# FFN output projection in three passes: each pass scaled and added onto the residual rows in DRAM by adding DMAs, in place of load, sum and store of a running sum

## The chip, the core and the metric

The kernel runs on one core of one Trainium2 chip. The metric is the device time of one execution in microseconds (us); lower is better. The engines are named as in the profile: PE (matrix multiplication, PEld its weight loads), DVE (vector), ACT (scalar, activation), POOL (GpSimd) and SP (which here only issues DMAs). DMAs issued on SP use the hardware queue q1, DMAs issued on POOL the software queue q0; both are carried out by the same 16 DMA engines.

## The reference

One layer of a decoder trunk on 512 tokens of width 2048, in float32. Its feed-forward half is what the change touches:

```
h   = rmsnorm(x, ffn_norm_g)               # x: the residual after the attention half, "x1"
hid = h @ w_ffn_in                         # 2048 -> 2 x 5632
x   = x + (silu(gate) * up) @ w_ffn_out    # 5632 -> 2048; the result is "x2"
ple = p @ w_ple
x   = x + sigmoid(rmsnorm(x, ple_norm_g) @ w_ple_gate) * ple
```

## The kernel before

Everything is held transposed, features on the 128 partitions and the 512 tokens along the free dimension. A row tile is 128 x 1024 float32 (512 KB): two blocks of 128 features. The residual x has 8 such tiles (`KU` = 8, index j), the hidden activations 22 (index u).

**Matmuls.** Each float32 operand is split into a high and a low part in fp32r, and each product is three matmuls (high x high, high x low, low x high). Two neighbouring units of 256 x 256 features can be multiplied by a Strassen scheme with 7 products ("S") or plainly with 8 ("P"). `pair(forms, ...)` computes one output row tile j from a list of operand forms: it takes the weights of one or two units at a time (`next_weights`), multiplies, and collects the result from the PSUM banks. `Pair.mix` and `mix_doubled` (L721, L754) combine the seven products into a `wide()` tile named `out` (two buffers, `bufs=2`) while the last unit runs. `Pair.out()` returns that tile (for pairs of plain units alone, it copies two PSUM banks into it on ACT, L792; for mixed pairs, it joins two PSUM banks on DVE, L799). `Pair.onto(h)` adds the result onto a tile h on DVE instead (L804 from `out`, or L808 twice straight from PSUM for plain pairs).

**Weights.** `Weights` loads the four blocks of an S unit by two SP DMAs (L329, L331), forms two differences by an adding DMA on POOL (L351, 256 KB, from DRAM onto SBUF), sums on DVE (L363) and splits into high parts on ACT (`whi`, L347) and low parts on DVE (`wlo`, L344). P units come by one SP DMA (L327). Four landing buffers and three slots of split weights turn round. The order is set by `tick()`, a small planner that is called twice per double unit: `after(n, fn)` runs fn n ticks later.

**Forms.** The operands on the moving side are forms: a row tile is loaded (L504), split on ACT (L274) and DVE (L275), with sums on DVE (L513). The raw tiles are blocks of one arena, `wholes`; the split forms live in an arena `parts` with room for eight S forms. A form of the next pass can be built only where both have room, and it is fetched from DRAM when `wholes` has. The engines' order in the built program follows from a list scheduler that honours these steps.

**The feed-forward output.** The hidden size is 5632, that is 22 units, too many forms for `parts`, so `w_ffn_out` is applied in three passes c = 0, 1, 2 over 8, 8 and 6 units (`PASSES`). In each pass, j runs over the 8 output tiles; at j = 0 (all units) and j = 1 (half of them, or in the last pass all four S units) units run as plain ones while the rest of their forms is still built. Between the passes the running sum of tile j is kept in DRAM (`spill["sum", j]`): pass 0 stores it (SP, L1436); pass 1 loads it, adds with `onto`, and stores it (L1441); pass 2 loads it and tile j of x1, adds with `onto`, scales the sum by the norm's row `row2` with `scaled` (DVE, L1224), adds x1 (DVE, L1444), stores x2 (L1445) and adds its squares to the next norm (`norm3.add`: ACT L956, DVE L960). The x2 tiles are loaded again as forms of the last stage, the gate (`w_gate`).

Of the kernel before, what the change touches and what calls it, by code (L numbers as in the profile page):

```python
# [12 lines left out]
F32 = mybir.dt.float32  # L13
F32R = mybir.dt.float32r
AF = mybir.ActivationFunctionType
ALU = mybir.AluOpType
# [3 lines left out]
P = 128  # L20
# [12 lines left out]
PASSES = "SSSSSSSS", "SSSSSSSS", "SSSSPP"  # L33
# [34 lines left out]
def hybrid_layer(  # L68
# [18 lines left out]
    nc = tc.nc  # L87
# [9 lines left out]
    def nm(s):  # L97
        return f"{s}_{next(names)}"
# [14 lines left out]
    class Arena:  # L113
# [5 lines left out]
        def take(self, n, how="low"):  # L119


            spots = []
            for start, size in self.holes:
                end = start + size
                if how == "place":
                    start = -(-start // (2 * PLACE)) * 2 * PLACE
                if end - start >= n:
                    if how == "high":
                        spots.append((-end, end - n))
                    elif how != "old":  # L130
                        spots.append((start, start))
                    else:
                        spots.extend((self.given[a // P : -(-(a + n) // P)].max(), a)
                                     for a in {*range(start, end - n + 1, 256), end - n})
            at = min(spots)[1]
            start, size = next(h for h in self.holes if h[0] <= at < h[0] + h[1])
            self.holes.remove((start, size))
            self.holes.extend(
                h for h in ((start, at - start), (at + n, start + size - at - n)) if h[1])
            return Block(self, at, n)  # L140

        def give(self, block):
            self.turns += 1
            self.given[block.start // P : -(-(block.start + block.n) // P)] = self.turns
            holes = sorted(self.holes + [(block.start, block.n)])
            self.holes = holes[:1]
            for s, n in holes[1:]:
                if sum(self.holes[-1]) == s:
                    self.holes[-1] = (self.holes[-1][0], self.holes[-1][1] + n)
                else:  # L150
                    self.holes.append((s, n))
# [42 lines left out]
    def after(n, fn):  # L194
        heapq.heappush(waiting, (clock[0] + n, next(names), fn))
# [306 lines left out]
    def load(src, n=1024, how="old"):  # L502
        b = take(n, how)
        nc.sync.dma_start(out=b.f(0, 1024), in_=src)  # L504
        return b
# [304 lines left out]
    def pair(forms, last=False, j=0, until=None, parts_done=None, at=0,  # L810
             home=lambda: None, doubled=0):

        until = until or (0,) * len(forms)
        kinds = now("".join(f.kind for f in forms), until, j)
        p = Pair(kinds, home, doubled)
        for k, n in doubles(kinds, at):
            slot, ws = next_weights()
            fs = forms[k : k + n]  # L820
            p.add(kinds[k], ws, [f.plain() if j < until[k] else f.get() for f in fs])
            for f, m in zip(fs, until[k : k + n]):
                if j == m - 1:
                    f.use_plain()
                if last:
                    f.free()
            slots.append(slot)
            if parts_done and k + n == kinds.find("P"):
                last_parts(p, forms[k + n :], parts_done)
                break  # L830
        return p
# [390 lines left out]
    def scaled(o, row):  # L1222
        b = o.rearrange("p (b t) -> p b t", t=T)
        nc.vector.tensor_tensor(out=b, in0=b, in1=row.unsqueeze(1).to_broadcast([P, 2, T]),  # L1224
                                op=ALU.mult)
# [10 lines left out]
    def block(w, i):  # L1236

        if w == "k":
            return a_tile("k", 1024)
        if w == "s":  # L1240
            y_a[i] = take(1024)
            return y_a[i].f()
# [56 lines left out]
    for n, ((w, i), pr) in enumerate(zip(order, made())):  # L1299
# [6 lines left out]
        o = pr.out(block(w, i) if n < 3 else None)  # L1306
# [29 lines left out]
    for j in range(KU):  # L1336
        for b in "ba":
# [9 lines left out]
            pr = pair([ys[b, i] for i in range(4)], last=j == KU - 1)  # L1347
# [4 lines left out]
            else:  # L1352
# [5 lines left out]


    norm2 = Norm()  # L1360
    spill = {(n, j): tc.dram_tile([P, 1024], F32, name=nm(n)) for n in ("x1", "sum", "x2")
             for j in range(KU)}
    there = set()

# [7 lines left out]
    for j in range(KU):  # L1372
# [5 lines left out]
        pr = pair(ms, last=j == KU - 1)  # L1378
# [3 lines left out]
        h = raw.popleft()  # L1382
# [13 lines left out]
    hs = []  # L1396
# [13 lines left out]
    for m in range(KH):  # L1410
        if m == KH - 1:
            builds.extend(hs[0])
        o = pair(fs, last=m == KH - 1, j=m, until=(1,) * KU, doubled=7).out()
        if m == 0:
            row2 = norm2.row()
# [6 lines left out]
    norm3 = Norm()  # L1422
    at = 0
    for c, units in enumerate(hs):
        first, at = at, at + len(units)
        if c == len(hs) - 1:
            builds.extend(gs)
        for j in range(KU):
            if j == KU - 1 and c < len(hs) - 1:
                builds.extend(hs[c + 1])  # L1430
            before = load(spill["sum", j]) if c else None
            x1 = load(spill["x1", j]) if c == len(PASSES) - 1 else None
            pr = pair(units, last=j == KU - 1, j=j, until=PLAIN_UNTIL[c], at=first,
                      doubled=7)
            if before is None:
                nc.sync.dma_start(out=spill["sum", j], in_=pr.out())  # L1436
                continue
            h = before.f()
            pr.onto(h)
            if x1 is None:  # L1440
                nc.sync.dma_start(out=spill["sum", j], in_=h)  # L1441
            else:
                scaled(h, row2)
                nc.vector.tensor_tensor(out=h, in0=h, in1=x1.f(), op=ALU.add)  # L1444
                nc.sync.dma_start(out=spill["x2", j], in_=h)  # L1445
                there.add(("x2", j))
                norm3.add(before)
                give(x1)
            give(before)


    for j in range(KU):
        e, x2 = load(ple_spill[j]), load(spill["x2", j])
# [21 lines left out]
        else:  # L1475
            o = pair(gs, j=j, until=GATE_UNTIL).out()
# [90 lines left out]
```

## Time and profile before

| | |
|---|---|
| median of 3 runs | 2690.93 us (2689.34 to 2696.23) |
| the profiled execution | 2691.74 us, of which the span of the instructions is 2690.0 us |
| mean granted clock of PE | 0.998 |
| PE busy | 2653.3 us, 99% of the span |
| DVE busy | 2207.7 us, 82% |
| ACT busy | 1388.7 us, 52% |
| POOL busy | 458.2 us, 17% |
| DMA | 548.62 MB moved |

By the times of its `sum` stores and loads, pass 0 of the FFN output runs from about 2060 to 2225 us of the span, pass 1 to about 2395, pass 2 to about 2525; the gate follows to the end at 2690. A busy PE in these tables is one that has a matmul in flight; the time in which it has none is what the waits of PE list. Lines such as L1224 are line numbers of the kernel before; the changed kernel's lines behind L1428 are some numbers lower.

### The profile page before, as it was taken

To read this page: it belongs to the slowest core of one execution; us is meant where nothing else is said; L and a number is where in the kernel's file an instruction comes from. 1 tells how busy PE (TensorE), PEld (TensorE's weight loads), DVE (VectorE), ACT (ScalarE), POOL (GpSimd) and SP (SyncE) were. 2 spreads that over 40 slices of the span, in tenths; PEclk is the share of its full clock that TensorE was granted. 3 is DMA by queue.
4 is the path that set the end of the run, shared out by engine and by line. 5 is a ranking of instruction groups with operands and counts; after the bars stand their busy time and mean duration, and the time that the engine had idled before them with its cause. 6 is when DMAs were issued, how large, how long until landed. Compare 5 with 4: busy or idle time off the path is not lost.

```text
span 2690.0 us, 42553 instructions
## 1 busy us (share of the span) xinstructions
PE 2653.3 (99%) x15496; PEld 2325.7 (86%) x15496; DVE 2207.7 (82%) x3715; ACT 1388.7 (52%) x2161; POOL 458.2 (17%) x549
## 2 busy tenths in 40 slices
PE   8999999999999999999999999999999999999999
PEld 7889898889898889988888888888888888888898
DVE  8687878787887666688898888888899889889876
ACT  7656565655554334375444444444445444444543
POOL 0223323232220000001111111111110111100010
PEclk9999999999999999999999999999999999999999
DMA  7677777777776457667888888888888979978884
GB/s 226 154 185 175 182 173 184 172 183 198 174 187 196 140 164 211 178 210 198 230 212 213 204 202 200 201 206 199 207 197 244 259 213 279 259 254 259 257 248 126
DMA packets 288241, 548.62 MB, mean 204 GB/s; under 512 B 25888, under 2 KB 138272, under 8 KB 288032
## 3 DMA queue, kind: packets, MB, share of 16 engines
q1 hardware_dynamic: 229232, 441.03, 50.3%
q0 software_dynamic: 58800, 104.88, 25.2%
q8 instruction: 121, 1.98, 0.3%
q14 instruction: 88, 0.72, 0.1%
HBM read 498.63 MB, written 47.19 MB: 203 GB/s over the span
## 4 chain that ended last, share of the span: by engine, by line
PE 85%; DVE 7%; DMA 3%; ACT 2%; issue 2%; POOL 1%; SPq 0%; DVEq 0%; ACTq 0%; POOLq 0%
PE ps L695 47%; PE ps L285 10%; PE ps L286 10%; PE ps L284 10%; PE small L695 6%; DVE wlo L344 2%; DVE out L754 1%; DMA wholes<-x 1%; DVE parts L275 1%; PE small L1157 1%; DMA wholes<-hid 1%; DVE wholes L363 1%; ACT whi L347 1%; DVE wholes L513 1%; PE small L1032 1%
## 5 line engine op out<-in xcount | busy, mean ns | idle before, releaser
L695 PE MATMUL ps<-parts,whi 128*128 128x512 f32 x3960 | 1324.8, 397 | 0.3 <-DVE p L754 0.3
L347 ACT ACTIVATE whi<-wholes 128x512 fp32r<-128x512 f32 (+3 forms) x933 | 866.0, 942 | 787.0 <-DVE wholes L363 274.0
L344 DVE TENSOR_TENSOR wlo<-wholes,whi 128x512 fp32r<-128x512 f32 (+3 forms) x933 | 974.1, 1078 | 85.6 <-ACT whi L347 85.4
L695 PEld LDWEIGHTS ps<-parts,wlo 128*128 128x128 f32 x3960 | 743.7, 188 | 168.1 <-issue 1.0
L695 PE MATMUL ps<-parts,wlo 128*128 128x256 f32 x3960 | 784.3, 279 | 0.1
L285 PE MATMUL ps<-parts,whi 128*128 128x256 f32 (+1 forms) x2070 | 679.5, 329 | 4.8 <-DVE parts L275 4.7
L284 PE MATMUL ps<-parts,whi 128*128 128x256 f32 (+1 forms) x2048 | 668.1, 328 | 12.4 <-ACT parts L274 10.6
L286 PE MATMUL ps<-parts,wlo 128*128 128x256 f32 (+1 forms) x2070 | 677.6, 329 | 1.7 <-DVE wlo L344 1.7
L695 PEld LDWEIGHTS ps<-parts,whi 128*128 128x128 f32 x3960 | 637.8, 189 | 5.9 <-issue 1.0
L285 PEld LDWEIGHTS ps<-parts,whi 128*128 128x128 f32 x2070 | 393.6, 190 | 46.5 <-DVE parts L275 7.3
L284 PEld LDWEIGHTS ps<-parts,whi 128*128 128x128 f32 x2048 | 388.5, 190 | 48.9 <-ACT parts L274 12.7
L286 PEld LDWEIGHTS ps<-parts,wlo 128*128 128x128 f32 x2070 | 393.5, 190 | 36.2 <-DVE wlo L344 3.2
L363 DVE TENSOR_TENSOR wholes<-wholes 128x256 f32<-128x256 f32 (+1 forms) x806 | 338.9, 420 | 19.1 <-issue 1.7
L754 DVE TENSOR_TENSOR out<-out,ps 128x256 f32<-128x256 f32 x460 | 190.8, 417 | 150.9 <-ACT out L751 150.2
L351 POOL DMA_DIRECT2D wholes<-w_ffn_in x172 | 150.1, 872 | 689.1 <-DVE wholes L363 251.7
L351 POOL DMA_DIRECT2D wholes<-w_in x132 | 118.3, 898 | 484.4 <-DMA wholes<-w_in 133.7
L695 PE MATMUL small<-parts,whi 128*128 128x512 f32 x440 | 174.5, 397 | 0.0
L275 DVE TENSOR_TENSOR parts<-wholes,parts 128x1024 fp32r<-128x1024 f32 (+4 forms) x134 | 131.0, 989 | 17.6 <-ACT parts L274 17.6
L274 ACT ACTIVATE parts<-wholes 128x1024 fp32r<-128x1024 f32 (+4 forms) x134 | 112.9, 865 | 46.9 <-DVE wholes L513 26.1
L351 POOL DMA_DIRECT2D wholes<-w_ffn_out x64 | 55.8, 872 | 402.5 <-DMA wholes<-w_ffn_out 101.6
L751 ACT ACTIVATE out<-ps 128x256 f32<-128x256 f32 x243 | 91.4, 385 | 47.5 <-PE ps L695 44.0
L1403 ACT ACTIVATE out<-out 128x512 f32<-128x512 f32 x44 | 27.9, 633 | 156.3 <-DVE out L1402 156.3
(120 smaller groups left out, 1721.6 us busy)
## 6 DMA issues: line engine op xcount, KB each, us to landing
wholes<-w_ffn_in SPq DMA_DIRECT2D x172, 384.0 KB, 5.6
wholes<-w_in SPq DMA_DIRECT2D x132, 384.0 KB, 5.0
wholes<-w_ffn_in SPq DMA_DIRECT2D x172, 256.0 KB, 4.8
wholes<-w_ffn_in POOLq DMA_DIRECT2D x172, 256.0 KB, 5.5
wholes<-w_in SPq DMA_DIRECT2D x132, 256.0 KB, 4.2
wholes<-w_in POOLq DMA_DIRECT2D x132, 256.0 KB, 4.9
wholes<-w_ffn_out SPq DMA_DIRECT2D x64, 384.0 KB, 5.4
wholes<-hid SPq DMA_DIRECT2D x42, 512.0 KB, 5.8
```

The costliest lines, as they stand in the source:

```text
L274: return (nc.scalar.activation(hi, src, AF.Copy), nc.vector.tensor_tensor(out=lo, in0=src, in1=hi.bitcast(F32), op=ALU.subtract))
L275: nc.vector.tensor_tensor(out=lo, in0=src, in1=hi.bitcast(F32), op=ALU.subtract))
L284: nc.tensor.matmul(ps, sh, mh, start=start, stop=False)
L285: nc.tensor.matmul(ps, sh, ml, start=False, stop=False)
L286: return nc.tensor.matmul(ps, sl, mh, start=False, stop=stop)
L344: in_turn(nc.vector.tensor_tensor(out=self.lo[:, blocks], in0=r, in1=h.bitcast(F32), op=ALU.subtract))
L347: in_turn(nc.scalar.activation(h, r, AF.Copy))
L351: nc.gpsimd.dma_start(out=raw[:, 3:5], in_=self.src[:, 1:3], accum_op=ALU.add)
L363: in_turn(nc.vector.tensor_tensor(out=o, in0=x, in1=y, op=ALU.add))
L695: m = nc.tensor.matmul(out, l, r, start=first and k == 0, stop=last and k == 1)
L751: in_turn(nc.scalar.activation(out, x, AF.Copy, scale=scale))
L754: in_turn(nc.vector.tensor_tensor(out=out, in0=x, in1=y, op=op))
```

## The change

Since the scale `row2` is the same for every pass, each pass's own result can be scaled and added to x1. There is no `sum` tile any more. In passes 0 and 1, the result `o` of tile j is scaled in place in its `out` buffer, and two ticks later a POOL DMA adds it onto x1's tile j in DRAM (512 KB, from SBUF onto DRAM). In pass 2, tile j of x1 (which now holds the first two passes) is loaded, the scaled result is added to it on DVE, and the rest is as before.

```diff
@@ spill
-    spill = {(n, j): tc.dram_tile([P, 1024], F32, name=nm(n)) for n in ("x1", "sum", "x2")
+    spill = {(n, j): tc.dram_tile([P, 1024], F32, name=nm(n)) for n in ("x1", "x2")
              for j in range(KU)}
@@ for c, units in enumerate(hs): ... for j in range(KU):
-            before = load(spill["sum", j]) if c else None
-            x1 = load(spill["x1", j]) if c == len(PASSES) - 1 else None
+            end = c == len(hs) - 1
+            h = load(spill["x1", j]) if end else None
             pr = pair(units, last=j == KU - 1, j=j, until=PLAIN_UNTIL[c], at=first,
                       doubled=7)
-            if before is None:
-                nc.sync.dma_start(out=spill["sum", j], in_=pr.out())
+            o = pr.out()
+            scaled(o, row2)
+            if not end:
+                after(2, lambda o=o, j=j: nc.gpsimd.dma_start(
+                    out=spill["x1", j], in_=o, accum_op=ALU.add))
                 continue
-            h = before.f()
-            pr.onto(h)
-            if x1 is None:
-                nc.sync.dma_start(out=spill["sum", j], in_=h)
-            else:
-                scaled(h, row2)
-                nc.vector.tensor_tensor(out=h, in0=h, in1=x1.f(), op=ALU.add)
-                nc.sync.dma_start(out=spill["x2", j], in_=h)
-                there.add(("x2", j))
-                norm3.add(before)
-                give(x1)
-            give(before)
+            nc.vector.tensor_tensor(out=h.f(), in0=h.f(), in1=o, op=ALU.add)
+            nc.sync.dma_start(out=spill["x2", j], in_=h.f())
+            there.add(("x2", j))
+            norm3.add(h)
+            give(h)
```

On POOL, before, the 64 adding DMAs of `w_ffn_out`'s weights stand in one row:

```order
L351 DMA wholes<-w_ffn_in 128x512 x172
L351 DMA wholes<-w_ffn_out 128x512 x64
```

With the change, the adds onto x1 (named `x_<number>`; L1438 is the new line) stand between them, here those of the first five tiles of pass 0:

```order
L351 DMA wholes<-w_ffn_in 128x512 x172
L351 DMA wholes<-w_ffn_out 128x512 x5
L1438 DMA x_823_9210<-out_18831 128x1024
L351 DMA wholes<-w_ffn_out 128x512 x4
L1438 DMA x_824_9211<-out_18901 128x1024
L351 DMA wholes<-w_ffn_out 128x512 x3
L1438 DMA x_825_9212<-out_19175 128x1024
L351 DMA wholes<-w_ffn_out 128x512 x4
L1438 DMA x_826_9213<-out_19351 128x1024
L351 DMA wholes<-w_ffn_out 128x512 x4
L1438 DMA x_827_9214<-out_19527 128x1024
```

Sixteen DMAs of 512 KB are thus queued on POOL among the weights' own adds, about one for every four of these.

On ACT, at the start of pass 2, before (`parts` are the forms' high parts, `whi` the weights'; L956 is the square of tile 1 for the norm, L718 a step of `mix` of tile 2):

```order
L347 ACTIVATE whi_78<-wholes 128x1024
L274 ACTIVATE parts<-wholes 128x4x256
L347 ACTIVATE whi_76<-wholes 128x1280
L956 ACTIVATE out_21774<-wholes 128x1024
L274 ACTIVATE parts<-wholes 128x4x256 x2
L718 ACTIVATE out_21839<-ps_21781 128x512
L347 ACTIVATE whi_76<-wholes 128x512
L718 ACTIVATE out_21839<-ps_21794 128x512
```

and with the change (L792 copies tile 1's PSUM banks into `out`):

```order
L508 ACTIVATE wholes<-wholes,gcol 128x512 x2
L274 ACTIVATE parts<-wholes 128x4x256
L792 ACTIVATE out_21774<-ps_21660 128x512
L347 ACTIVATE whi_78<-wholes 128x1024
L792 ACTIVATE out_21774<-ps_21661 128x512
L508 ACTIVATE wholes<-wholes,gcol 128x512 x2
L347 ACTIVATE whi_76<-wholes 128x1280
L956 ACTIVATE out_21780<-wholes 128x1024
L718 ACTIVATE out_21845<-ps_21786 128x512
L347 ACTIVATE whi_76<-wholes 128x512
L718 ACTIVATE out_21845<-ps_21799 128x512
```

The two form splits (`128x4x256 x2`) that stood directly behind the square of tile 1 are no longer there, and two copies of PSUM banks have come in ahead of it.

On SP, at the step from pass 1 to pass 2, before (`hid` tiles are numbered in the order of the units; 10849 is the last unit, u = 21, and 10844 is u = 16, the first of pass 2, whose second load this is; an S form is loaded twice, once for its plain part and once for its sums):

```order
L327 DMA wholes<-w_ffn_out 128x1024 x2
L504 DMA wholes<-hid_10848 128x1024
L504 DMA wholes<-sum_9218 128x1024
L327 DMA wholes<-w_ffn_out 128x1024
L329 DMA wholes<-w_ffn_out 128x2x256
L331 DMA wholes<-w_ffn_out 128x768
L504 DMA wholes<-x_823_9210 128x1024
L1441 DMA sum_9225<-wholes 128x1024
L329 DMA wholes<-w_ffn_out 128x2x256
L331 DMA wholes<-w_ffn_out 128x768
L504 DMA wholes<-hid_10849 128x1024
L504 DMA wholes<-hid_10844 128x1024
```

and with the change (the numbers are 8 lower, since the 8 `sum` tiles are gone: 10841 is u = 21, 10837 to 10839 are u = 17 to 19):

```order
L327 DMA wholes<-w_ffn_out 128x1024 x5
L504 DMA wholes<-hid_10837 128x1024
L504 DMA wholes<-x_823_9210 128x1024
L327 DMA wholes<-w_ffn_out 128x1024
L329 DMA wholes<-w_ffn_out 128x2x256
L331 DMA wholes<-w_ffn_out 128x768
L504 DMA wholes<-hid_10840 128x1024
L504 DMA wholes<-hid_10841 128x1024
L504 DMA wholes<-hid_10838 128x1024
L329 DMA wholes<-w_ffn_out 128x2x256
L331 DMA wholes<-w_ffn_out 128x768
L504 DMA wholes<-hid_10839 128x1024
```

The stores and loads of `sum` are gone. The second loads of u = 17, 18 and 19 now stand here, about four weight loads earlier than before, and that of u = 16 stands in the middle of pass 1; the loads of u = 20 and 21 stand next to each other at nearly the place where u = 21 stood.

## The prediction

> **What bounds the kernel now.** I read the page first, then the windows of the FFN output and the gate, then the waits of PE, and last the timeline at the gaps of PE.
>
> ```profile
> PE 2653.3 (99%) x15496; PEld 2325.7 (86%) x15496; DVE 2207.7 (82%) x3715; ACT 1388.7 (52%) x2161; POOL 458.2 (17%) x549
> 2060.00:2225.00 165.00, 164.99 (x922) 143.12 (x921) 145.50 (x251) 82.60 (x109) 22.69 (x26) 1.00 0.87 254
> 2225.00:2395.00 170.00, 166.53 (x925) 143.53 (x924) 149.69 (x251) 77.53 (x102) 22.69 (x26) 1.00 0.89 260
> 2395.00:2600.00 205.00, 197.16 (x1218) 177.94 (x1218) 176.61 (x261) 107.39 (x138) 21.41 (x23) 0.98 0.85 261
> ```
>
> The windows give span, PE, PEld, DVE, ACT, POOL, clock, DMA share and GB/s. PE bounds the kernel: it is busy for 99% of the span. In pass 0 (the first window) it never stops, in pass 1 it loses 3.5 us, from pass 2 on more. The change touches no matmul, so whatever it gains or loses must pass through the time in which PE has nothing to do. That time, from the start of pass 0 to the end of the kernel, stands in the waits of PE (us in total, times, longest):
>
> ```profile
> PE ps L284 <- ACT parts L274: 5.3, 4, 2.0
> PE ps L285 <- DVE parts L275: 4.2, 4, 2.0
> PE ps L286 <- DVE wlo L344: 1.0, 1, 1.0
> PE small L944 <- DVE diag L942: 0.8, 1, 0.8
> ```
>
> 11.3 us in all, and 9.5 of them are waits for forms (L274, L275), not for weights. PE's gaps at the step from pass 1 to pass 2, and the one wait for weights, in the timeline (start, duration, and in brackets the idle time before):
>
> ```profile
> 2390.92 0.73 PE L284 MATMUL ps<-parts,whi 128*128 128x512 f32 x2 [1.52 <-ACT parts L274]
> 2419.66 0.62 PE L284 MATMUL ps<-parts,whi 128*128 128x256 f32 x3 [2.04 <-ACT parts L274]
> 2421.31 0.39 PE L285 MATMUL ps<-parts,whi 128*128 128x256 f32 x1 [0.32 <-DVE parts L275]
> 2423.33 0.62 PE L284 MATMUL ps<-parts,whi 128*128 128x256 f32 x3 [1.05 <-ACT parts L274]
> 2424.59 0.39 PE L285 MATMUL ps<-parts,whi 128*128 128x256 f32 x1 [0.64 <-DVE parts L275]
> 2463.22 0.39 PE L286 MATMUL ps<-parts,wlo 128*128 128x256 f32 x1 [1.02 <-DVE wlo L344]
> ```
>
> After the group at 2420 the granted clock drops, and again near 2565:
>
> ```profile
> 2426.00:2430.00 4.00, 4.00 (x17) 3.46 (x17) 3.93 (x8) 3.66 (x6) 0.00 (x0) 0.66 0.91 315
> 2564.00:2570.00 6.00, 5.87 (x36) 5.88 (x37) 4.75 (x7) 2.12 (x2) 0.00 (x0) 0.72 0.71 223
> ```
>
> That is 4 x 0.34 = 1.4 us and 6 x 0.28 = 1.7 us of clock lost. So no change in these stages can gain more than 11.3 + 3.1 = 14.4 us.
>
> **The change part by part.** *PE's gaps at 2420 to 2425* (4.05 us in the four rows). What PE waits for are second halves of pass 2's S forms, needed at j = 2. This is the row of engines behind them:
>
> ```profile
> 2408.28 0.38 SPq L504 DMA_DIRECT2D wholes<-hid  x1
> 2414.62 1.22 DVE L1224 TENSOR_TENSOR wholes<-wholes 128x1024 f32<-128x1024 f32 x1
> 2416.36 1.21 DVE L1444 TENSOR_TENSOR wholes<-wholes 128x1024 f32<-128x1024 f32 x1
> 2417.60 1.06 ACT L956 ACTIVATE out<-wholes 128x1024 f32<-128x1024 f32 x1 [3.52 <-DVE wholes L1444]
> 2418.57 1.04 ACT L274 ACTIVATE parts<-wholes 128x1024 fp32r<-128x1024 f32 x1
> 2422.22 1.06 ACT L274 ACTIVATE parts<-wholes 128x1024 fp32r<-128x1024 f32 x1 [2.62 <-DVE wholes L513]
> ```
>
> The last second half is requested from DRAM only at 2408.3, and ACT, which works in order, stands 3.5 us at the square L956, which waits for scale and x1's addition on DVE; the form's split is queued behind it. In the changed order both reasons are gone: the second loads of units 17 to 19 stand about four weight loads earlier (pass 0 has 32 of them in 165 us, 5.2 us each, so some 20 us), because `wholes` no longer holds a block for `sum`, and no split of a form stands right behind tile 1's square. I take the whole 4.05 us and the clock's 1.4 us: -5.4. The bounds are 0 (another step is just as late) and -5.4. For the clock, the Trainium skill says otherwise ("TensorE: Matmul & The Clock Gate", section "Why this matters for your kernels"): it asks only that PE have no idle gaps over about 3 us. Here single gaps of at most 2.04 us were enough; by the page's rule the clock would owe nothing to these gaps, and this term would be 4.05. The trace differs, and I go by it.
>
> *The gap at 2390.92* (1.52) waits for the split of unit 21, loaded just before it is needed; in the new order that load stands one weight load earlier at most, with unit 20's directly ahead of it. I take no gain; bounds -1.5 and +1.5. *The gap at 2463.22* (1.02) is a low part that DVE delivers late, with the following operations of tile j on DVE; I take it as gone, -1.0, bounds 0 and -1.0.
>
> *DVE.* The durations are those of the same shapes in pass 2 and in pass 1:
>
> ```profile
> L1444 DVE TENSOR_TENSOR wholes<-wholes 128x1024 f32<-128x1024 f32 x8 | 9.8, 1222 | 0.1
> L1224 DVE TENSOR_TENSOR wholes<-wholes 128x1024 f32<-128x1024 f32 x8 | 9.8, 1220 | 0.1
> L804 DVE TENSOR_TENSOR wholes<-wholes,out 128x1024 f32<-128x1024 f32 x6 | 7.3, 1220 | 0.0
> L808 DVE TENSOR_TENSOR wholes<-wholes,ps 128x512 f32<-128x512 f32 x3 | 2.0, 684 | 0.5 <-PE ps L286 0.5
> L792 ACT ACTIVATE out<-ps 128x512 f32<-128x512 f32 x2 | 1.2, 588 | 1.5 <-PE ps L286 1.5
> ```
>
> Pass 0 gains eight scales, 8 x 1.22 = 9.8 us; pass 1 has a scale for each L804, the same 1.22; pass 2 loses six L804 and two pairs of L808, 6 x 1.22 + 4 x 0.68 = 10.0 us, while ACT gets 2 x 0.59 for each plain tile of passes 1 and 2, in which ACT is half idle. So DVE's sum stays, but pass 0 rises from 145.5 to 155.3 of 165 us. What covers it is the lead of DVE's low parts on PE. Pass 1 already does the same work per tile with DVE at 99.61 of 110 us and PE does not stop once:
>
> ```profile
> 2085.00:2110.00 25.00, 25.00 (x132) 21.11 (x131) 23.68 (x43) 13.30 (x20) 3.49 (x4) 1.00 0.97 304
> 2270.00:2380.00 110.00, 110.00 (x624) 95.66 (x623) 99.61 (x171) 53.04 (x72) 15.54 (x18) 1.00 0.86 247
> ```
>
> The first of these rows is the place where the cover is thin: at j = 1 and 2 of pass 0, DVE has 1.3 us of 25 free. Two scales (tiles 0 and 1) fall in there: 2.44 us against 1.3 free. I take +1.5, bounds 0 and +2.4.
>
> *DMA.* The queues in pass 0 (packets, MB, share of 16 engines) the landing times there, and the POOL instruction that issues a weight's add (mean 873 ns):
>
> ```profile
> q1 hardware_dynamic: 15749, 34.82, 60.0%
> q0 software_dynamic: 3780, 6.88, 26.4%
> wholes<-w_ffn_out POOLq DMA_DIRECT2D x26, 256.0 KB, 5.6
> sum<-out SPq DMA_DIRECT2D x8, 512.0 KB, 3.4
> L351 POOL DMA_DIRECT2D wholes<-w_ffn_out x52 | 45.4, 873 | 288.0 <-DMA wholes<-w_ffn_out 101.6 <-DVE out L754 67.5 <-DVE wlo L344 28.4
> ```
>
> On q1 a megabyte takes 0.600 x 165 / 34.82 = 2.84 us of all engines, on q0 0.264 x 165 / 6.88 = 6.33 us. A 512 KB (0.524 MB) store or load of `sum` thus cost 1.5 us, an adding DMA of this size 3.3 us if it goes by bytes; if it goes by packets (0.184 us each at 8 per engine) 1.5 us. No row shows an add onto DRAM; I take 3.3, the nearest kind. Pass 0 then rises by 8 x 1.8 = 14.6 us to a share of 0.96; pass 1 by 8 x (3.3 - 3.0) = 2.4 us; pass 2 falls by 8 x 1.5 = 12 us. An average share of 0.97 did not stop PE in the window from 2085 to 2110, so I put the sum at +0.5 us, bounds 0 and the second rival.
>
> *POOL and SP.* POOL takes 0.87 us to issue an add and is busy for 22.69 of 165 us in pass 0; the x1 add comes two ticks behind its scale, so it does not hold POOL up, and the two `out` buffers are wanted again only two tiles (2 x 165 / 8 = 41 us) later. SP loses 32 issues. Both 0. The x1 loads of pass 2 wait for adds of pass 1 that ended a pass earlier: 0.
>
> Sum: -5.4 - 1.0 + 1.5 + 0.5 = -4.4 us. The profiled execution took 2691.74 us, 0.8 more than the median of 2690.93, so the forecast on the median is 2690.9 - 4.4 = 2686.5 us.
>
> **The rivals.** *First, every gap goes.* With more free room in `wholes` and a lighter DVE in pass 2, the other form waits (at the start of pass 1 and in the gate) may close too. For it: 9.5 of 11.3 us are form waits, and the x2 chain (scale, add, store, reload as a form) is one DVE operation shorter. Against it: at the start of pass 1, DVE has no less to do. The price is 14.4 us of gains, less 1 to 5 for what cannot close: 2677 to 2682.
>
> *Second, weights fall behind the x1 adds (slower).* The weights' adds L351 are issued on the same POOL queue as the x1 adds. One that is issued right behind such an add lands later by the add's time, 3.3 us on top of 5.6. In the Trainium skill ("DMA: Bandwidth & Descriptors", section "Queues, rings and completion order") each DMA engine serves one queue's ring in order and takes turns only between queues; by that rule the wait is the whole of the add's time. The trace shows that some lateness is covered:
>
> ```profile
> ACT whi L347 <- DMA wholes<-w_ffn_out: 17.5, 6, 6.0
> 2385.64 1.06 ACT L347 ACTIVATE whi<-wholes 128x1024 fp32r<-128x1024 f32 x1 [6.04 <-DMA wholes<-w_ffn_out]
> ```
>
> ACT waited six times for late weights in passes 0 and 1, once for 6 us, and PE never waited for weights there (its one wait for `wlo` in the table above is the one at 2463). But there the waits came singly; here it is one double unit in four, sixteen times. It decides from the point at which an add onto DRAM takes more than about 5 us of the engines, because the 3.3 us are within the cover and 6 us are its largest proof. At 6.6 us (reading and writing DRAM twice as slow as the add onto SBUF) and 5 us covered, 16 x 1.6 = 26 us less the 4 gained: 2712. At half of that, 2699.
>
> *Third, the gaps move.* The step to pass 2 keeps as many late forms, only others (units 20 and 21 are loaded side by side, at the last moment): 2688 to 2694, no change.
>
> **How the numbers follow.** A measurement of this kernel can tell about 0.3%, 8.1 us, from no change: faster is below 2682.9, slower above 2699.0. I give the forecast (2683 to 2688) 0.46, the gaps that move 0.14, every gap closed 0.20, the weights behind the adds 0.20. This makes faster 0.20, same 0.60, slower 0.20. The range reaches from 2677, where every gap is closed, to 2702, which holds the beginning of the second rival; some 0.04 is left out below and 0.14 above.
>
> **What would show it.** In the changed profile: PE's waits on L274 and L275 around 2420 gone and the clock at 1.00 behind them; no PE wait on `wlo` in passes 0 and 1 apart from 1 to 2 us near 2100; L1438 landing in 6 to 9 us, and L351 at up to 9. The forecast is wrong if PE waits for `wlo` or `whi` at regular distances of one tile (about 20 us) in passes 0 and 1, or if L1438 takes over 10 us, or if passes 0 and 1 (335 us in the windows) become longer by more than 5 us.

## The result, and the profile after

| | before | after |
|---|---|---|
| median of 5 runs | 2690.98 us (2689.34 to 2696.23) | 2677.87 us (2674.32 to 2683.39) |
| the profiled execution | 2691.74 us, span 2690.0 us | 2676.21 us, span 2674.5 us |

The ratio is 0.9953, 95% interval 0.9942 to 0.9964: the change makes the kernel 0.47% faster, 13.1 us by the medians and 12.6 us by the ratio. The forecast was 2686.5 us and "no change"; the measured time lies in the range (2677 to 2702), 0.9 us above its lower end. It is the time of the first rival, every gap closed. By the prediction's own bound (2682.9 us) this is the case "faster", which it gave a chance of 0.20.

The busy times on the page of the changed kernel, and the windows of pass 0, of pass 1, and of pass 2 with the gate's start (columns as before: span, PE, PEld, DVE, ACT, POOL, clock, DMA share, GB/s):

```profile
PE 2647.8 (99%) x15496; PEld 2322.1 (87%) x15496; DVE 2206.1 (82%) x3720; ACT 1392.0 (52%) x2171; POOL 471.2 (18%) x565
2060.00:2225.00 165.00, 164.88 (x921) 142.81 (x920) 154.34 (x260) 83.15 (x110) 29.87 (x34) 1.00 0.93 246
2225.00:2395.00 170.00, 169.10 (x939) 146.07 (x938) 153.67 (x260) 82.95 (x109) 29.84 (x34) 1.00 0.90 243
2395.00:2600.00 205.00, 204.38 (x1319) 186.26 (x1318) 172.13 (x264) 110.58 (x147) 23.50 (x25) 1.00 0.83 252
```

PE now stops for 0.1, 0.9 and 0.6 us in the three windows, where before it lost 0.0, 3.5 and 7.8. The waits of PE from 2060 us to the end (us in total, times, longest), all of them:

```profile
PE ps L284 <- ACT whi L347: 0.5, 1, 0.5
PE ps L285 <- DVE parts L275: 0.4, 1, 0.4
PE small L944 <- DVE diag L942: 0.3, 1, 0.3
PE ps L286 <- DVE wlo L344: 0.3, 1, 0.3
```

1.5 us, with smaller ones 1.65, against 11.3 before: 9.7 us are gone. The windows behind the two places where the granted clock had dropped (0.66 and 0.72 before):

```profile
2424.00:2430.00 6.00, 5.72 (x48) 5.52 (x48) 6.00 (x9) 3.87 (x5) 0.24 (x1) 1.00 1.02 322
2564.00:2570.00 6.00, 6.00 (x49) 5.84 (x48) 5.49 (x9) 1.85 (x4) 1.80 (x2) 1.00 0.91 272
```

The clock stays at 1.00. A drop before was 6 us x 0.28 = 1.7 us of PE's time (in the window from 2564), that is 3.4 us at half clock; two of them make 3.4 us. 9.7 + 3.4 = 13.1 us, which is also the difference of the medians. That the two agree so closely is partly luck: waits and drops are read from the two profiled executions, which are 15.5 us apart, and 2.4 us of these stand in no wait or drop listed here.

What made the forms arrive in time is visible on SP. The last load of a hidden tile for pass 2, in the timeline of the changed kernel (start, duration):

```profile
2382.67 0.54 SPq L504 DMA_DIRECT2D wholes<-hid  x1
```

Before the change it stood at 2408.28. It now stands 26 us earlier in the span, in front of the first tile of pass 2.

### The profile page after: what moved, and what is told of

It reads as the page before. It is cut to its first block, busy times and chain, and to the rows that moved or that the text cites. A ratio compares the mean times of both kernels' runs of the same rounds, so it can differ in the third digit from the quotient of the medians.

```text
span 2674.5 us, 42586 instructions
## 1 busy us (share of the span) xinstructions
PE 2647.8 (99%) x15496; PEld 2322.1 (87%) x15496; DVE 2206.1 (82%) x3720; ACT 1392.0 (52%) x2171; POOL 471.2 (18%) x565
## 3 DMA queue, kind: packets, MB, share of 16 engines
q8 instruction: 121, 1.98, 0.3%
## 4 chain that ended last, share of the span: by engine, by line
PE 89%; DVE 5%; ACT 2%; DMA 2%; issue 1%; POOL 1%; SPq 0%; DVEq 0%; ACTq 0%; POOLq 0%
PE ps L695 48%; PE ps L286 11%; PE ps L285 11%; PE ps L284 11%; PE small L695 6%; DVE wlo L344 1%; DVE out L754 1%; PE small L1157 1%; DMA wholes<-x 1%; PE small L1032 1%; DVE wholes L363 1%; ACT whi L347 1%; DVE parts L275 0%; PE small L1107 0%; POOL wholes L1120 0%
## 5 line engine op out<-in xcount | busy, mean ns | idle before, releaser
L754 DVE TENSOR_TENSOR out<-out,ps 128x256 f32<-128x256 f32 x460 | 190.5, 416 | 142.1 <-ACT out L751 141.8
L351 POOL DMA_DIRECT2D wholes<-w_ffn_in x172 | 150.1, 872 | 690.0 <-DVE wholes L363 268.5
L351 POOL DMA_DIRECT2D wholes<-w_in x132 | 117.8, 894 | 480.6 <-DVE wholes L363 125.9
L275 DVE TENSOR_TENSOR parts<-wholes,parts 128x1024 fp32r<-128x1024 f32 (+4 forms) x138 | 131.5, 965 | 18.9 <-ACT parts L274 18.9
L351 POOL DMA_DIRECT2D wholes<-w_ffn_out x64 | 55.9, 873 | 355.2 <-DMA wholes<-w_ffn_out 87.6
L751 ACT ACTIVATE out<-ps 128x256 f32<-128x256 f32 x243 | 91.0, 384 | 46.6 <-PE ps L695 43.3
```

The source lines that it names most:

```text
L275: nc.vector.tensor_tensor(out=lo, in0=src, in1=hi.bitcast(F32), op=ALU.subtract))
L351: nc.gpsimd.dma_start(out=raw[:, 3:5], in_=self.src[:, 1:3], accum_op=ALU.add)
L751: in_turn(nc.scalar.activation(out, x, AF.Copy, scale=scale))
L754: in_turn(nc.vector.tensor_tensor(out=out, in0=x, in1=y, op=op))
```

## The experiments

Each kernel was timed in five rounds beside the kernel before on the same chip. The last two columns are the sum of PE's waits from 2060 us on in the profiled execution, and how often the granted clock fell to half there (not counting the end of the kernel). The profiled execution is one of those timed and need not be the median one: for the block really occupied and for each add issued twice it was the fastest. "Above after" is (ratio - 0.9953) x 2691 us; with intervals of about ±0.0011 on both ratios, differences below some 4 us are not told apart.

The theory is room: the running sum's block of `wholes`, with its transfers, is what made the forms late, and the change frees it. The rival is DVE: what counts is that DVE does 10 us less in pass 2. A third question is the price of the adds, on which the second rival of the prediction rests.

| kernel | median us | ratio to before [95%] | above after, us | PE waits, us | drops |
|---|---|---|---|---|---|
| before | | 1 | 12.6 | 11.3 | 2 |
| after | 2677.87 | 0.9953 [0.9942, 0.9964] | 0 | 1.65 | 0 |
| block of `wholes` held, with the sum's transfers | 2695.33 | 1.0012 [1.0003, 1.0021] | 15.9 | 12.3 | 2 |
| block put aside in the planning only | 2683.69 | 0.9972 [0.9961, 0.9984] | 5.1 | 6.7 | 0 |
| block really occupied, no transfer | 2687.86 | 0.9981 [0.9973, 0.9990] | 7.5 | 9.0 | 1 |
| extra stores in pass 1 | 2681.30 | 0.9964 [0.9950, 0.9978] | 3.0 | 5.8 | 0 |
| extra stores in passes 1 and 2 | 2690.70 | 1.0001 [0.9991, 1.0011] | 12.9 | 9.5 | 2 |
| extra copies in passes 0 and 1 | 2692.24 | 0.9998 [0.9988, 1.0007] | 12.1 | 11.8 | 3 |
| DVE +1.22 us per tile of pass 2 | 2682.82 | 0.9968 [0.9955, 0.9980] | 4.0 | 6.5 | 0 |
| DVE +1.22 us per tile of pass 0 | 2683.34 | 0.9965 [0.9952, 0.9978] | 3.2 | 5.0 | 1 |
| each add issued twice | 2688.01 | 0.9984 [0.9976, 0.9993] | 8.3 | 6.1 | 0 |
| adds left out | 2676.85 | 0.9946 [0.9933, 0.9958] | -1.9 | 3.2 | 1 |
| load, add on DVE, store instead of the adding DMA | 2709.99 | 1.0070 [1.0057, 1.0083] | 31.5 | 23.2 | 4 |
| before, with the sum loaded late | 2688.79 | 0.9990 [0.9981, 0.9999] | | 9.2 | 2 |

### All of the sum's block put back

```diff
...
+            held = load(xT[j]) if c else None
...
             if not end:
...
+                if held:
+                    nc.vector.tensor_copy(held.f(0, 1), o[:, 0:1])
+                    nc.sync.dma_start(out=spill["sum", j], in_=held.f())
+                    give(held)
                 continue
...
+            nc.vector.tensor_copy(held.f(0, 1), o[:, 0:1])
+            give(held)
```

> The changed kernel, with one block of wholes taken per tile of passes 1 and 2 as before: it is loaded from DRAM (an input tile) before the pair, and in pass 1 stored to an unused DRAM tile behind it; the result does not use it, DVE copies one column into it. Room theory (the gaps of PE closed because no block of wholes is bound to a sum, so hidden tiles are fetched earlier): PE's waits for forms come back, 8 to 11 us with 1 or 2 drops of the clock, 2687 to 2692 us. DVE theory (the gaps closed because DVE has one operation of 1.22 us less per tile in pass 2): no change against the changed kernel, 2676 to 2680 us, PE waits under 3 us.

2695.33 us, 3 us above the upper end of what room should give: with the block and its transfers back the whole gain is gone, though scale and adding DMA stay. The waits of PE, and two gaps in its timeline:

```profile
PE ps L284 <- ACT parts L274: 6.4, 3, 3.4
PE ps L285 <- DVE parts L275: 2.6, 3, 1.1
2396.50 0.93 PE L284 MATMUL ps<-parts,whi 128*128 128x512 f32 x2 [3.42 <-ACT parts L274]
2427.50 0.73 PE L284 MATMUL ps<-parts,whi 128*128 128x256 f32 x2 [2.63 <-ACT parts L274]
```

These are the waits of before, on the same lines at the same step between the passes, and the clock drops behind both. So the gain does not come from the adding DMA as such, but from what it makes needless.

### The block put aside in the planning, and one really occupied

```diff
+            held = take(1024, "old") if c else None
...
+                if held:
+                    give(held)
...
```

> The changed kernel, with one block of wholes per tile of passes 1 and 2 taken from the arena and given back behind the tile, but neither loaded nor stored. In the built order the first loads of pass 2's hidden tiles stay early (as in the changed kernel), the second loads stand about three weight loads later. Room theory, if the bare place in the arena is what counts: about half of the gain lost, 2681 to 2686 us. If it is the block's load and store (the transfers, and the wait for the store before the place is used again): 2676 to 2680 us. DVE theory: 2676 to 2680 us.

2683.69 us, within the first expectation. Here nothing writes or reads the block, so only the planner sees less room: the first loads keep their early places, and 5 us are lost. In the second kernel the block is in use from the tile's start to its end:

```diff
+            held = take(1024, "old") if c else None
+            if held:
+                nc.gpsimd.memset(held.f(0, 1), 0.0)
...
+                if held:
+                    nc.vector.tensor_copy(held.f(0, 1), o[:, 0:1])
+                    give(held)
...
```

> The changed kernel, with a block of wholes occupied in each tile of passes 1 and 2 from a tiny memset of one of its columns by GpSimd to a tiny copy by VectorE at the tile's end: room without any transfer. In the built order the first loads of the hidden units 16 to 19 stand behind 55, 59, 63 and 67 weight loads, as before the change, not behind 43 to 47. If room and the order of the loads cost the time: 2688 to 2695 us, waits of PE of 8 to 12 us, the clock drops at about 2425 again. If the transfers cost it: 2679 to 2684 us, as with the block that was only put aside.

2687.86 us, 7.5 us above the changed kernel: just under the lower edge of what room alone should give, with waits of the size expected for it (9.0 us) and one clock drop, at 2391 instead of 2425. The timeline of SP, ACT and PE shows the chain, and the last two rows a gap at the start of pass 1 and a wait of POOL:

```profile
2380.59 0.53 SPq L504 DMA_DIRECT2D wholes<-hid  x1
2388.86 1.06 ACT L274 ACTIVATE parts<-wholes 128x1024 fp32r<-128x1024 f32 x1 [9.99 <-DMA wholes<-hid]
2389.97 0.51 PE L284 MATMUL ps<-parts,whi 128*128 128x512 f32 x1 [2.17 <-ACT parts L274]
...
2409.28 0.42 SPq L504 DMA_DIRECT2D wholes<-hid  x1
...
2231.32 0.38 PE L285 MATMUL ps<-parts,whi 128*128 128x256 f32 x1 [1.05 <-DVE parts L275]
...
POOL wholes L1435 <- issue: 22.7, 3, 18.3
```

A hidden tile is requested at 2380.59, ACT stands 9.99 us for it, and PE 2.17 us for ACT; the last request stands at 2409.28, as before the change (2408.28). No byte is moved more than in the changed kernel. That room sets when the forms are fetched, and that this costs PE time, is shown. POOL also stands idle ahead of the memset (L1435), once for 18.3 us, with the weights' adds queued behind it. The profile names nothing that ends this wait ("issue"); that the memset waits for its block is likely, not shown. So the 7.5 us are an upper end for room alone.

### The sum's transfers without its block

```diff
...
             h = load(spill["x1", j]) if end else None
+            if c:
+                nc.sync.dma_start(out=spill["sum", j], in_=spill["x1", j])
```

> The changed kernel, with a copy of 512 KB from x1's rows into an unused DRAM tensor at the start of each tile in passes 1 and 2: transfers of the size of the sum's, but no block of wholes, and the loads of hidden units stay at the changed kernel's early places. If the block's room is what costs, 2677 to 2680 us, and PE's waits from 2060 us on stay below 3 us. If the transfers of sum are what costs (the DMA share falls by 16 loads and 16 stores, and that let the forms arrive in time), the copies bring most of it back: 2686 to 2692 us, with waits of PE of 7 us or more.

It cost 12.1 us, but not where it was meant to: the copies wait for nothing but the add of the pass before, and were issued from 2086.0 to 2401.9 us, in passes 0 and 1, beside the adds. It shows another way to lose time, below, and does not price the old transfers. So stores of the result, which come at the right time, took their place:

```diff
...
+            for to in ("sum", "sum2")[:(0, 2, 1)[c]]:
+                nc.sync.dma_start(out=spill[to, j], in_=o)
```

> The changed kernel, with each tile's scaled result also stored to unused DRAM rows, twice in pass 1 and once in pass 2: as many transfers of 512 KB, in the same passes, as the loads and stores of the sum had there before the change, but no block of wholes, and the loads of hidden units stay early. The copies of the earlier run lay in passes 0 and 1, beside the adds, and so did not answer the question. If transfers at these places are what cost: 2684 to 2692 us, with late weights (the wait of the split L347 for w_ffn_out well above the changed kernel's 22.3 us) and PE waits of 6 us or more. If room and the order of the loads are what cost: 2676 to 2680 us, PE waits below 4 us.

2690.70 us. By the total this speaks for the transfers, but the profile says where the time went. The window of pass 1, and a wait of ACT in pass 2:

```profile
2225.00:2395.00 170.00, 167.46 (x930) 144.34 (x929) 154.13 (x259) 81.83 (x108) 28.90 (x33) 1.00 0.97 284
ACT out L718 <- DMA sum<-out: 12.3, 5, 3.3
```

In pass 1 PE lost 1.6 us more than in the changed kernel (169.10), at a DMA share of 0.97 instead of 0.90. In pass 2 the extra store held an `out` buffer, and ACT stood 12.3 us for it. To separate the two, the next kernel has the stores of pass 1 alone (the edit is shown against the kernel just described):

```diff
-            for to in ("sum", "sum2")[:(0, 2, 1)[c]]:
+            for to in ("sum", "sum2")[:(0, 2, 0)[c]]:
```

> The run before, with the two extra stores in pass 1 alone. There it lost only about 1.6 us of PE's time at a DMA share of 0.97; in pass 2 the extra store also held an out buffer (ACT's L718 waited 12.3 us for it), which is a wait of its own and no price of a transfer. If the transfers of pass 1 are a main part: 2684 to 2690 us. If the 12.8 us of the run before came from the out buffer in pass 2, and the transfers cost what PE lost in pass 1: 2678 to 2681 us, and the waits of PE behind 2395 us stay as in the changed kernel, below 3 us.

2681.30 us, at the upper end of the second expectation (2681), 3 us above the changed kernel with intervals that overlap. In pass 1 PE lost 2.9 us, 2.0 more than in the changed kernel, and in the window from 2395 to 2600 it lost 2.8 us, 2.2 more. So the transfers of pass 1 are worth some 3 us, known to 4. Most of the loss of the run before came with the store in pass 2. ACT's wait for the `out` buffer is what the profile shows of it; the price of that store's transfer alone is not separated from it. What the load of the sum cost in pass 2 without its block, no run shows.

### DVE's share

```diff
                 continue
+            nc.vector.tensor_tensor(out=o, in0=o, in1=o, op=ALU.max)
             nc.vector.tensor_tensor(out=h.f(), in0=h.f(), in1=o, op=ALU.add)
```

> The changed kernel with one more DVE operation of 128x1024 (1.22 us) per tile of pass 2 between the scale and the addition of x1 (the maximum of the result with itself, which leaves it as it is): DVE has as much to do in pass 2 as before. DVE theory: the gaps near 2420 and 2463 and in the gate come back, 2684 to 2690 us. Room theory: under 2 us, 2676 to 2681 us, PE waits under 4 us from pass 2 on.

2682.82 us, between the two expectations. Eight operations of 1.22 us in pass 2, the amount that the change takes off DVE there, bring back 4.0 us, at the limit of what can be told. The forms are loaded as early as in the changed kernel; what returns are waits of PE on DVE's parts:

```profile
PE ps L285 <- DVE parts L275: 3.1, 4, 1.3
PE ps L286 <- DVE wlo L344: 1.9, 3, 1.3
PE ps L284 <- ACT parts L508: 0.9, 1, 0.9
```

The same operation in pass 0:

```diff
             scaled(o, row2)
+            if not c:
+                nc.vector.tensor_tensor(out=o, in0=o, in1=o, op=ALU.max)
```

> The changed kernel, with one more VectorE operation of 1.22 us on each tile's result in pass 0, 9.8 us in all, right behind the scale: a second dose of the load that the change put there. By my term for DVE (each tile's operation beyond what DVE has free at 2085 to 2110 us delays PE; DVE is busy for 24.75 of these 25 us now) two operations cost 2.4 us there, and the rest, at 154 + 10 of 165 us, a little more: 2680 to 2684 us, with PE waits on VectorE (L275, L344, L754) of 3 to 6 us in the first 165 us. If the lead of VectorE's low parts on PE is long, nothing is seen: 2676 to 2679 us.

3.2 us, the interval overlapping that of the changed kernel. The thin place of the prediction, in the changed kernel and with the second dose:

```profile
2085.00:2110.00 25.00, 24.89 (x134) 20.99 (x133) 24.75 (x43) 13.06 (x19) 4.39 (x5) 1.00 0.98 296
```
```profile
2085.00:2110.00 25.00, 24.27 (x125) 19.81 (x124) 24.93 (x45) 12.83 (x18) 3.74 (x5) 1.00 0.88 262
PE small L944 <- DVE diag L942: 2.6, 1, 2.6
```

The change filled DVE to 24.75 of 25 us and cost PE 0.1 us there; the next dose costs 0.73 us there. The rest of its loss in the profile is one wait at the gate, L944, with a clock drop behind it. That wait was 0.8 us before, 0.3 after, and 2.1 us in the kernel without adds, so it says little about pass 0. The time lies in the first expectation (2680 to 2684) by luck: in place of 3 to 6 us of waits in pass 0 there are 0.7.

### The adds

```diff
...
-                after(2, lambda o=o, j=j: nc.gpsimd.dma_start(
-                    out=spill["x1", j], in_=o, accum_op=ALU.add))
+                for to in ("x1", "x0"):
+                    after(2, lambda o=o, j=j, to=to: nc.gpsimd.dma_start(
+                        out=spill[to, j], in_=o, accum_op=ALU.add))
```

> The changed kernel, with each adding DMA issued twice: the second goes onto a copy of x1's rows that nobody reads (the stage before stores this copy too, 8 stores more). If an add onto DRAM of 512 KB takes less of the engines than the 3.3 us that I costed, and POOL has room for 0.9 us more per tile, nothing is seen: 2677 to 2681 us, no wait of PE for wlo in passes 0 and 1. If the second rival's mechanism is real and only its price was too high, a double add (twice 3.3 us and more ahead of a weight's add) passes the 5 us of cover: 2684 to 2700 us, with PE waiting for wlo or whi about once per tile.

```diff
-                after(2, lambda o=o, j=j: nc.gpsimd.dma_start(
-                    out=spill["x1", j], in_=o, accum_op=ALU.add))
```

> The changed kernel without the adding DMAs: the scaled results of passes 0 and 1 are not added to x1's rows, so the output lacks them. It prices the 16 adds on the path: if they cost nothing where they stand, 2675 to 2679 us; if the weights' adds behind them are late by some of their time without PE showing it as a wait, 2668 to 2674 us.

Without the adds 2676.85 us, within the error the same as with them. The profile agrees more closely: PE loses as much without the adds in pass 0 (0.12 us) and in pass 1 (0.90 us) as with them, so sixteen adds cost nothing where they stand. A second add behind each costs 8.3 us. Pass 1 without adds, and the wait of ACT's splits for weights from DRAM, from 2060 to 2395 us, without adds, in the changed kernel and with double adds:

```profile
2225.00:2395.00 170.00, 169.10 (x939) 146.30 (x938) 155.74 (x262) 83.05 (x109) 22.62 (x26) 1.00 0.79 218
ACT whi L347 <- DMA wholes<-w_ffn_out: 6.4, 4, 3.3
```
```profile
ACT whi L347 <- DMA wholes<-w_ffn_out: 22.3, 12, 5.0
```
```profile
ACT whi L347 <- DMA wholes<-w_ffn_out: 65.7, 23, 6.6
PE ps L695 <- DVE p L754: 3.8, 3, 1.4
```

With double adds the weights are late three times as long as in the changed kernel (17.5 us before the change), and the cover is used up.

Which weights the adds make late is told by the landing times from 2060 to 2395 us, of a load that SP issues (384 KB) and of the add L351 that POOL issues on the same queue as the adds onto x1: without adds, in the changed kernel, with double adds.

```profile
wholes<-w_ffn_out SPq DMA_DIRECT2D x53, 384.0 KB, 5.0
wholes<-w_ffn_out POOLq DMA_DIRECT2D x52, 256.0 KB, 5.4
```
```profile
wholes<-w_ffn_out SPq DMA_DIRECT2D x53, 384.0 KB, 6.6
wholes<-w_ffn_out POOLq DMA_DIRECT2D x52, 256.0 KB, 5.5
```
```profile
wholes<-w_ffn_out SPq DMA_DIRECT2D x52, 384.0 KB, 7.5
wholes<-w_ffn_out POOLq DMA_DIRECT2D x51, 256.0 KB, 6.4
```

In the median, the sixteen adds of the changed kernel delay the loads on the other queue by 1.6 us and those on their own queue by 0.1. In the changed kernel's trace only 5 of the 52 weights' adds are issued while an add onto x1 is still on its way.

With double adds PE does not show the lateness as a wait for `wlo` or `whi`, though, but on the read-out of its banks (L754). How that comes about is seen best in the kernel with the extra copies:

```profile
2111.63 1.27 ACT L347 ACTIVATE whi<-wholes 128x1280 fp32r<-128x1280 f32 x1 [3.42 <-DMA wholes<-w_ffn_out]
2112.81 0.91 ACT L751 ACTIVATE out<-ps 128x256 f32<-128x256 f32 x3
2113.20 0.75 DVE L754 TENSOR_TENSOR out<-out,ps 128x256 f32<-128x256 f32 x2 [0.77 <-ACT out L751]
2113.68 0.50 PE L695 MATMUL ps<-parts,whi 128*128 128x512 f32 x1 [1.98 <-DVE out L754]
```

ACT stands 3.42 us for a late weight; the copies out of PSUM (L751) are queued behind that split, DVE's sums wait for them, and PE for the bank.

### The adding DMA undone, scale kept

```diff
-            h = load(spill["x1", j]) if end else None
+            h = load(spill["x1", j])
...
+            nc.vector.tensor_tensor(out=h.f(), in0=h.f(), in1=o, op=ALU.add)
...
-                after(2, lambda o=o, j=j: nc.gpsimd.dma_start(
-                    out=spill["x1", j], in_=o, accum_op=ALU.add))
+                nc.sync.dma_start(out=spill["x1", j], in_=h.f())
+                give(h)
                 continue
-            nc.vector.tensor_tensor(out=h.f(), in0=h.f(), in1=o, op=ALU.add)
```

> The changed kernel, with the adding DMA of passes 0 and 1 replaced by a load of x1's block, an addition on VectorE and a store: the same scaling of each pass, but a block of wholes held in every tile, 16 additions of 1.22 us more on VectorE, and 16 loads more. If the gain comes from the block that the adding DMA makes needless, this loses all of it and the extra VectorE work in pass 0 (155 + 10 of 165 us) is felt: 2695 to 2710 us, with waits of PE on low parts in pass 0. If the gain came from scaling each pass's result early (the short end of pass 2), most of it stays: 2677 to 2684 us.

2709.99 us, 31.5 us above the changed kernel, the upper end of the first case. The largest waits of PE:

```profile
PE ps L284 <- ACT parts L274: 11.0, 5, 3.7
PE ps L285 <- DVE parts L275: 6.9, 6, 2.3
```

Scaling early is no gain by itself: with the additions back on DVE and their block back in `wholes`, both at once here, nothing of the gain is left. The waits on low parts that were expected in pass 0 are small; those for forms are the large ones.

### The kernel before, with the sum loaded late

```diff
-            before = load(spill["sum", j]) if c else None
             x1 = load(spill["x1", j]) if c == len(PASSES) - 1 else None
...
+            before = load(spill["sum", j]) if c else None
             if before is None:
```

> The kernel before, with the load of the running sum moved behind the pair, so that its block of wholes is bound for a shorter time; the sum, the DVE work and the transfers are those of before. In the built order the last five hidden loads stand two to four weight loads earlier than before. Room theory: part of the gain, 2681 to 2687 us, with the gaps near 2420 smaller. DVE theory: 2689 to 2694 us, as before or slower, since the sum arrives later at DVE.

2688.79 us, between the two expectations: 2.7 us, at the edge of what can be told. The waits for forms at the step to pass 2 went, others came:

```profile
PE ps L286 <- DVE wlo L344: 4.9, 4, 2.0
PE ps L284 <- ACT whi L347: 2.4, 1, 2.4
```

That is the third rival (the gaps move), in another kernel. The time for which the block is held is not the whole cause.

## Why the prediction came out as it did

**The frame held.** Gain and loss passed through PE's waits and the clock behind them: 9.7 + 3.4 us of the ceiling's 11.3 + 3.1. That the time lies in the stated range is owed to the range, which was drawn to take in the first rival; the sum itself gave 4.4 us of the 13.1.

**The gaps at 2420 to 2425** went, and the first of the two reasons given is shown: the second loads stand 26 us earlier (20 forecast), and putting the block back brings gaps at this place back. The second reason, ACT's square in front of the form's split, was not undone by itself. Their clock drop was worth 1.7 us, not 1.4, so the term is 5.7 instead of 5.4. The page cited there ("TensorE: Matmul & The Clock Gate" of the Trainium skill, section "Why this matters for your kernels") asks for no idle gaps over about 3 us; with both drops gone together with gaps of at most 2.04 us, the trace differs from it as said. The clearer of the two is the drop behind the single gap of 2.00 us at 2564, since four gaps stand ahead of the other.

**The gap at 2463** (-1.0) went too; 0.3 us of waits for `wlo` is left.

**The step that failed** is the sentence on the gap at 2390.92, "I take no gain", and the silence on the others: the gaps at 2229, 2243, 2528 and 2564 (1.25 + 0.64 + 0.76 + 2.00 = 4.65 us) stand in no term of the sum, as if they stayed. Of all of them 0.4 us of waits for forms and 0.3 us for `diag` are left, and a wait of 0.5 us for `whi` has come in. The first rival had this case; the argument against it was that DVE has no less to do at the start of pass 1. That was the wrong resource there: with the block put aside or occupied, and DVE's scale unchanged, gaps of 0.9 to 1.3 us return at about 2230 (waits on L275), so it is room that had held these forms back. The gap at 2390.92 belongs to them: close to it PE waits again, for 3.42 us with the block and its transfers and for 2.17 us with the block occupied. What closed the gap at 2564, the largest of them (2.00 us, and 1.7 of the clock behind it), is open. The first rival's reason was an operation less in the x2 chain; DVE's extra operation in pass 2 puts one back, and the gaps that it brings (1.31 and 0.91 us) stand at other matmuls, at 2514 and 2524, near the gate's start. The matmul that waited at 2564 stands again only in the kernel with load, addition and store (2577.14, below), where pass 2 has no operation more than in the changed kernel. The missing terms are 1.5 + 4.65 us of waits, less 0.7, and a clock drop of 1.7: 7.2 us of the 8.7 between the forecast gain and the measured one. Most of the rest is what DVE and the DMAs were charged and did not take.

**DVE in pass 0** (+1.5, bounds 0 and +2.4) measured 0.1. The cover was there, and just there: 0.25 of 25 us are free now.

**DMA** (+0.5) measured 0 (PE's windows of passes 0 and 1 in the kernel without adds). The adds go over q0; its row on the page, before, after and with double adds:

```profile
q0 software_dynamic: 58800, 104.88, 25.2%
```
```profile
q0 software_dynamic: 61104, 113.27, 27.0%
x<-out POOLq DMA_DIRECT2D x16, 512.0 KB, 8.4
```
```profile
q0 software_dynamic: 63408, 121.66, 28.5%
```

0.270 x 2674.5 - 0.252 x 2690.0 = 44 us for 16 adds, 2.8 us of all engines for one (2.6 by the next step), between the two ends 1.5 and 3.3, nearer to the one by bytes, which the sum used. Landing 8.4 us lies in the 6 to 9 us named.

**The second rival** did not come, and its price condition was about right: one add of 2.8 us is within the cover, two in a row (about 5.5 us) are not and cost 8.3 us. Its mechanism is not what the traces show. L351, queued behind the adds, lands in 5.5 us with them and 5.4 without; it is SP's loads on the other queue that rise from 5.0 to 6.6 us, and with double adds both kinds rise by about 0.9 us more. The ring order that the rival drew from the Trainium skill ("DMA: Bandwidth & Descriptors", section "Queues, rings and completion order") is not refuted by this, since few weights' adds were issued with an add still ahead of them; but no run here shows that the delay is the whole time of the add ahead.

**Did each step get its share?** What was taken back alone: room 7.5 at most, transfers of pass 1 3.0, DVE of pass 2 4.0, together 14.5 us beside the 12.6 of the whole. Room and all transfers together are 15.9, some 5 us more than room and the transfers of pass 1 one by one, and no run shows where these stand. Each is known to some 4 us. That room held back the forms at the start of pass 1 and at the step to pass 2 is shown; what closed the gaps at 2463, 2528 and 2564 is not, and the split to the microsecond stays open.

## What to carry to other kernels

Where PE is busy for 99% and waits are short, list every wait from the change onward and ask of each which resource it waits for in the end (room, a transfer, an engine's queue); a change that frees room in an arena acts on all waits for loads into it, not only on those nearest to the edit. An adding DMA in place of load, addition and store pays through the buffer and the engine time that it makes needless, as long as the transfers beside it, on either queue, have lead enough to bear the delay. A copy that depends on nothing near it is issued where the scheduler likes, so a traffic experiment must show in the trace that its transfers lie where they were meant to.

## What the runs showed of the hardware

A single gap of PE of about 2 us was mostly enough for the granted clock to fall, and one of 1.5 us was not. Of before, the gap of 2.00 us at 2564 (the window behind it, at 0.72, is in the prediction) and the window behind the gap of 1.52 us at 2390.92; of the kernel with copies, the window behind its gap of 1.98 us; of the kernel with load, addition and store, an exception at 2.06 us:

```profile
2564.13 0.39 PE L285 MATMUL ps<-parts,whi 128*128 128x256 f32 x1 [2.00 <-DVE parts L275]
2391.00:2396.00 5.00, 5.00 (x22) 3.93 (x23) 4.43 (x8) 1.39 (x2) 0.00 (x0) 1.00 0.92 300
```
```profile
2112.00:2118.00 6.00, 4.32 (x16) 3.71 (x17) 5.15 (x11) 3.67 (x7) 0.88 (x1) 0.72 0.92 171
```
```profile
2577.14 0.39 PE L285 MATMUL ps<-parts,whi 128*128 128x256 f32 x1 [2.06 <-DVE parts L275]
2577.00:2583.00 6.00, 5.40 (x42) 5.09 (x42) 3.30 (x5) 1.49 (x4) 0.00 (x0) 1.00 0.93 257
```

Inside the drop behind 2564, before, the granted clock is half:

```profile
2565.50:2568.50 3.00, 3.00 (x16) 3.00 (x15) 3.00 (x4) 0.06 (x1) 0.00 (x0) 0.50 0.81 238
```

A drop thus lasts 3.4 us (6 x 0.28 / 0.5), so a gap of 2 us costs 3.7 with it. Gaps in a row prolonged it: behind three gaps of 2.40, 1.39 and 1.42 us from 2518 on, the kernel with the late sum ran 11 us at a mean of 0.53:

```profile
2519.00:2530.00 11.00, 8.19 (x40) 7.69 (x39) 8.13 (x16) 1.81 (x3) 2.56 (x2) 0.53 0.85 276
```
